# A hybrid decoder layer on one core: the recurrence's GELU, two weight sums, the turned rows and five joins in other places

## The chip, the cores and the metric

The kernel runs on one core of a Trainium2 chip. The metric is the device time of one execution in microseconds; where several runs of a kernel are given, their median stands. The engines are TensorE (PE, its weight loads PEld), VectorE (DVE), ScalarE (ACT), GpSimd (POOL), and SyncE (SP), which here issues most transfers.

## The reference

One layer of a decoder on 512 tokens of width 2048, in float32. Two mixers run side by side on the normalized input: a gated linear recurrence of 1024 channels behind a short convolution, and a head group of RWKV type (16 heads of 64). Then come a gated feed-forward net of width 6144 with a convolution over three tokens in its gate, a gated embedding, and a last norm:

```
xb = causal_dwconv(z[..., :D_LRU], conv_a_w, conv_a_b)
yb = gelu(z[..., D_LRU:2 * D_LRU])
out_a = rmsnorm(rg_lru(xb, ...) * yb, lru_norm)
...
h = h + concatenate([out_a, out_b], -1) @ w_o
u = rmsnorm(h, ln_ffn)
gate = causal_dwconv(u @ w_gate, conv_f_w, conv_f_b)
h = h + (gelu(gate) * (u @ w_up)) @ w_down
u = rmsnorm(h, ln_ple)
e = sigmoid(u @ w_ple_gate) * (p @ w_ple_proj)
h = h + rmsnorm(e, ln_ple_post)
return rmsnorm(h, ln_final)
```

## The kernel before

Every large product is made of three matmuls on two halves of the float32 operands: a weight tile `wraw` or `x` is split into `whi` (ScalarE, L138) and the rest `wlo` (VectorE, L139), and TensorE sums high times high, low times high and high times low. Where a weight is a sum of blocks (below), the sum comes first.

Phase 1 holds the mixers. It is written as generators whose pieces a scheduler orders by priority: `high_priority(offset=...)` moves an instruction up on the engines. For each of 4 head groups of the recurrence two blocks (i = 0, 1) of 128 channels pass through `lru_y` (L1013). Its dense product goes into a PSUM bank of two, named `mm`. VectorE empties the bank into `y` (L1021), ScalarE takes the GELU (L1022), and for i = 0 the gates' matmuls follow (L1031 to L1035), each emptied by ScalarE (L1038). Then come the exponential, tanh and square root of the recurrence (L1044 to L1046), POOL's product (L1050), VectorE's scan (L1051) and the product with `y` (L1052), which goes to `oa` in DRAM (L1053) and is read back later as `row` and `lx`. GELU, square root and exponential each need another table in ScalarE; a change shows as ACT_TABLE_LOAD. The head group's own chain (`Tm`, `MQ`, `NQ`, `Tt`) runs between these on all engines.

Phase 2 starts with the output projection, the hidden state `hT` and, in `forms`, the operands `s` of a fast product. The state goes to `hd` in DRAM (L1287). The gate loop makes 48 blocks n of 128 columns, gate (even n) and up (odd n), p = n // 2 being the pair. A block has seven units, named p1, p4, p2, q5, p7, p6 and p3, each one sub-product with a weight that is a block of `wgu` or a sum of some. `gate_order` (L1122) gives their order, `gate_unit` (L1132) their weights. Blocks are loaded into `x0` to `x7` by SP (L1139), sums are made by VectorE (`add`, L1143) or by a POOL transfer that accumulates into `g["s"]` (L1160). Between the units of the first blocks the token sums of `hT` squared are made (L1278, L1279, then a matmul L202, POOL's root L206, a broadcast L215).

A gate block is scaled (L1346) and convolved into the buffer x9 (ScalarE L1349, VectorE L1351, GELU L1352); the next up block is multiplied by it (L1433) and `spill` writes it out. The 16 rows of the hidden state are also turned here, for the later stages that want tokens on partitions: `row` is loaded from `hd` (L1414), transposed in place on 32 by 32 tiles (L1404) and written by four transfers to `hx` (L1407). One row is turned every 18 units from the 28th unit on.

After the down projection and the gated embedding the end handles four tiles tt of 128 tokens, in an order written by hand. The last gate product of each tile is on TensorE (L1590 to L1592); ScalarE and VectorE make its part of the embedding and its sums (L1699 to L1705), VectorE a mean (L1636), POOL a power (L1623). With the result r, `joined` (L1647) makes e r + h for four column blocks cb on VectorE (L1650), `rfin` (L1641 to L1644, again POOL's power) the last norm's factor, and `final` (L1652) scales each block, on ScalarE (L1655) or VectorE (L1657), and writes it out (L1658).

Of the kernel before, what the change touches and what calls it, by code (L numbers as in the profile page):

```python
# [7 lines left out]
ALU = mybir.AluOpType  # L8
# [82 lines left out]
class Builder:  # L91
# [921 lines left out]
    def lru_y(self, n, i):  # L1013
# [7 lines left out]
        V.tensor_tensor(y, ps, self.rs, ALU.mult)  # L1021
        SC.activation(y, y, AF.Gelu_apprx_tanh)  # L1022
# [17 lines left out]
        with self.tc.high_priority(offset=W['offl']):  # L1040
            tx, t1 = self.lgate[2 * i:2 * i + 2]

            rc = T("lrc")
            SC.activation(rc, t1, AF.Exp, scale=self.dv("m4sp", m), bias=self.dv("m4sp", m))  # L1044
            SC.activation(t1, t1, AF.Tanh, scale=self.dv("m2sp", m), bias=self.dv("m2sp", m))
            SC.activation(t1, t1, AF.Sqrt, scale=-0.25)  # L1046
            V.scalar_tensor_tensor(t1, rc, 1.0, t1, ALU.add, ALU.mult)
            G.memset(t1[:, 0:1], 0.5)
            V.scalar_tensor_tensor(tx, tx, 1.0, self.xc[i], ALU.add, ALU.mult)
            G.tensor_tensor(t1, t1, tx, ALU.mult)  # L1050
            V.tensor_tensor_scan(tx, rc, t1, 0.0, ALU.mult, ALU.add)  # L1051
            V.tensor_tensor(tx, tx, y, ALU.mult)  # L1052
            nc.sync.dma_start(self.oa[m], tx)  # L1053
            if m == 0:
                SC.activation(self.rsa, tx, AF.Square)
            else:
                SC.activation(rc, tx, AF.Square)
                V.tensor_tensor(self.rsa, self.rsa, rc, ALU.add)
# [72 lines left out]
    def gate_unit(self, n, u):  # L1131
# [22 lines left out]
        if u == "p7":  # L1154
            if n < 2:
                g[11] = load(2, 0, 0)
            return add(g[21], g[21], g[11])
        if u == "p6" and n in (0, NF - 1):
            return add(g["s"], g["s"], g[11])
        nc.gpsimd.dma_start(g["s"], src(0, 0 if u == "p6" else 1), accum_op=ALU.add)  # L1160
# [70 lines left out]
    def phase2(self):  # L1231
# [171 lines left out]
        def turn(m):  # L1403
            V.transpose(acc, acc)  # L1404
            for a in range(4):
                f = m % 4 * 128 + 32 * a
                nc.sync.dma_start(hx[m // 4][:, f:f + 32].rearrange("(b i) j -> i b j", i=32),  # L1407
                                  acc[32 * a:32 * a + 32].rearrange("i (b j) -> i b j", j=32))

        raw, c = [], None  # L1410
        for k, (n, u) in enumerate(self.gate_order()):
            m = k // 18 - 1
            if 0 <= m < KT and k % 18 == 6:
                nc.sync.dma_start(acc, hd[m // 2][:, m % 2])  # L1414
            if 0 <= m < KT and k % 18 == 10:
                turn(m)
# [3 lines left out]
            if n == 1 and u == "p6":  # L1420
                self.rstd_bcast(acc, D, RMS_EPS, k2, rs, rt)
                c = B(9)
                conv(0, o, c)
# [10 lines left out]
            raw.append(o)  # L1434
            if p % 2 == 1:
                spill(p // 2, raw)
                raw = []
# [213 lines left out]

        def final(tt, r, cb, act=True):  # L1652
            ix = tt * 4 + cb
            if act:
                SC.activation(e[ix], e[ix], AF.Copy, scale=r)  # L1655
            else:
                V.tensor_scalar(e[ix], e[ix], r, None, MU)  # L1657
# [30 lines left out]
        with self.tc.manual_schedule(engines={ET.PE, ET.DVE, ET.Activation, ET.Pool}):  # L1688
            for tt in range(4):
# [6 lines left out]

                sg, ee, x = T("e", 2, (128, 2, S))[:, 0], T("e", 2, (128, 2, S))[:, 0], e[tt * 4 + 3][:, last]
# [9 lines left out]
                if tt:  # L1707

                    joined(tt - 1, r, (3,))
                    for cb in range(4):  # L1710
                        final(tt - 1, rf, cb)
                r = rn
                joined(tt, r, (0,))
                rf = rfin(tt, r)
                joined(tt, r, (1, 2))
            joined(3, r, (3,))
            for cb in range(4):
                final(3, rf, cb, cb < 3)
# [67 lines left out]
```

## Time and profile before

| what | value |
|---|---|
| median of 3 runs | 2527.17 us (2523.64 to 2529.20) |
| the profiled execution's own time | 2528.72 us |
| its span (first to last instruction) | 2526.9 us |
| mean granted clock of TensorE | 0.992 |
| ScalarE's splits L138 of `x` | 332, mean 1061 ns |
| VectorE's splits L139 of `x` | 332, mean 1219 ns |
| accumulating transfers L1160 | 94 of 512 KB, median 5.7 us to land |

The profile is one execution. Each row of a timeline gives the start, the duration, the engine, the line, the operation, its output and inputs, and in brackets how long the engine had been idle and what ended that. A view of stretches gives the busy time of each engine in each, the clock that TensorE was granted (1.00 is full speed), and the share of its transfer engines that was busy. The rows on which the argument rests are in the prediction.

### The profile page before, as it was taken

What the parts mean: (1) busy time and instruction counts of PE and PEld (TensorE: products, weight loads), DVE (VectorE), ACT (ScalarE), POOL (GpSimd) and SP (SyncE); (2) the same over time, 40 slices, a digit from 0 to 9 for tenths busy, and PEclk for the clock granted to TensorE, in tenths of its full rate; (3) what the DMA queues carried; (4) which work ended last, traced back from release to release, by engine and by line L of the source; (5) the groups of instructions that cost most, each with busy time, mean ns of one, the idle gap of its engine ahead of it and who ended that gap; (6) DMA issues with size and microseconds to landing.
All of it is one profiled execution on the core that took longest, in us unless ns stands there. A gap on an engine that the chain in (4) does not pass through costs nothing.

```text
span 2526.9 us, 51719 instructions
## 1 busy us (share of the span) xinstructions
PE 2473.3 (98%) x21858; PEld 2182.3 (86%) x21858; DVE 1903.1 (75%) x2626; ACT 1250.0 (49%) x1735; POOL 220.3 (9%) x244
## 2 busy tenths in 40 slices
PE   9989999999999989999999999999999999999997
PEld 8867777777777889999999999999988888888887
DVE  5855775776585879878988888888877787896457
ACT  6563654556442545434444444444466454535345
POOL 0000100101031000000000000000000000000001
PEclk9999999999999999999999999999999999999998
DMA  7222222222342568888877777776788686853333
GB/s 260 89 78 63 88 77 65 88 81 68 102 131 93 161 198 218 203 212 221 211 196 176 204 194 193 203 196 176 213 250 234 172 264 188 254 130 117 100 92 109
DMA packets 168570, 402.17 MB, mean 159 GB/s; under 512 B 48529, under 2 KB 60817, under 8 KB 168337
## 3 DMA queue, kind: packets, MB, share of 16 engines
q1 hardware_dynamic: 133744, 307.62, 36.9%
q0 software_dynamic: 19872, 72.36, 17.3%
q10 hardware_dynamic: 14720, 18.88, 2.2%
q8 instruction: 171, 2.80, 0.5%
q14 instruction: 63, 0.51, 0.1%
HBM read 358.16 MB, written 40.63 MB: 158 GB/s over the span
## 4 chain that ended last, share of the span: by engine, by line
PE 60%; DVE 5%; DMA 3%; issue 2%; ACT 1%; POOL 0%; SPq 0%; POOLq 0%; ACTq 0%; DVEq 0%
PE mm L1304 7%; PE mm L1303 7%; PE mm L1302 7%; PE mm L1448 6%; PE mm L1447 6%; PE mm L1451 6%; PE wk L1302 3%; PE wk L1303 3%; PE wk L1304 3%; PE mm L1590 2%; PE mm L1591 2%; PE mm L1592 2%; PE mm L173 2%; PE mm L175 2%; PE mm L177 2%
## 5 line engine op out<-in xcount | busy, mean ns | idle before, releaser
L138 ACT ACTIVATE whi<-x 128x1024 fp32r<-128x1024 f32 x332 | 351.1, 1061 | 450.5 <-PE mm L1303 181.2
L139 DVE TENSOR_TENSOR wlo<-x,whi 128x1024 fp32r<-128x1024 f32 x332 | 404.7, 1219 | 120.4 <-ACT whi L138 116.5
L1302 PE MATMUL mm<-s,whi 128*128 128x256 f32 x1432 | 398.0, 278 | 4.5 <-ACT whi L138 3.6
L1304 PE MATMUL mm<-s,wlo 128*128 128x256 f32 x1432 | 398.3, 278 | 3.8 <-DVE wlo L139 3.7
L1303 PE MATMUL mm<-s,whi 128*128 128x256 f32 x1432 | 397.9, 278 | 0.0
L138 ACT ACTIVATE whi<-wraw 128x1024 fp32r<-128x1024 f32 (+1 forms) x223 | 227.0, 1018 | 341.7 <-PE mm L175 165.3
L139 DVE TENSOR_TENSOR wlo<-wraw,whi 128x1024 fp32r<-128x1024 f32 (+1 forms) x223 | 269.4, 1208 | 132.3 <-ACT whi L138 130.3
L173 PE MATMUL mm<-x,whi 128*128 128x512 f32 x832 | 332.5, 400 | 1.5 <-DVE hT L468 0.9
L177 PE MATMUL mm<-x,wlo 128*128 128x512 f32 x832 | 332.1, 399 | 0.0
L175 PE MATMUL mm<-x,whi 128*128 128x512 f32 x832 | 330.5, 397 | 0.0
L1302 PEld LDWEIGHTS mm<-s,whi 128*128 128x128 f32 x1432 | 270.6, 189 | 5.0 <-ACT whi L138 3.8
L1304 PEld LDWEIGHTS mm<-s,wlo 128*128 128x128 f32 x1432 | 270.0, 189 | 4.7 <-DVE wlo L139 4.7
L1303 PEld LDWEIGHTS mm<-s,whi 128*128 128x128 f32 x1432 | 270.1, 189 | 0.2
L1448 PE MATMUL mm<-whi,s 128*128 128x512 f32 x680 | 265.4, 390 | 0.9 <-DVE s L157 0.9
L1447 PE MATMUL mm<-whi,s 128*128 128x512 f32 x680 | 265.6, 391 | 0.0
L173 PEld LDWEIGHTS mm<-x,whi 128*128 128x128 f32 x832 | 157.1, 189 | 37.1 <-issue 2.7
L177 PEld LDWEIGHTS mm<-x,wlo 128*128 128x128 f32 x832 | 156.9, 189 | 34.0 <-issue 1.9
L175 PEld LDWEIGHTS mm<-x,whi 128*128 128x128 f32 x832 | 157.1, 189 | 33.7 <-issue 1.8
L1451 PE MATMUL mm<-wlo,s 128*128 128x512 f32 x680 | 181.3, 390 | 0.0
L1302 PE MATMUL wk<-s,whi 128*128 128x256 f32 x584 | 162.5, 278 | 2.0 <-ACT whi L138 2.0
L1304 PE MATMUL wk<-s,wlo 128*128 128x256 f32 x584 | 162.4, 278 | 0.4 <-DVE wlo L139 0.4
L1160 POOL DMA_DIRECT2D x<-wgu x94 | 82.7, 880 | 913.5 <-DVE wlo L139 663.9
(579 smaller groups left out, 5386.2 us busy)
## 6 DMA issues: line engine op xcount, KB each, us to landing
x<-wgu SPq DMA_DIRECT2D x144, 512.0 KB, 4.4
x<-wgu POOLq DMA_DIRECT2D x94, 512.0 KB, 5.7
wraw<-wz SPq DMA_DIRECT2D x80, 512.0 KB, 3.5
x<-wd SPq DMA_DIRECT2D x52, 512.0 KB, 6.0
wraw<-wgu SPq DMA_DIRECT2D x51, 512.0 KB, 4.6
x<-wd POOLq DMA_DIRECT2D x44, 512.0 KB, 6.0
wraw<-wpg SPq DMA_DIRECT2D x31, 512.0 KB, 3.5
rd<-x SPq DMA_DIRECT2D x24, 512.0 KB, 4.7
```

The source lines that it names most:

```text
L138: nc.scalar.activation(hi, raw, AF.Copy)
L139: nc.vector.tensor_tensor(lo, raw, hi.bitcast(F32), ALU.subtract)
L173: nc.tensor.matmul(ps, hi[:, k, :], xh, start=first and i == 0, stop=False)
L175: nc.tensor.matmul(ps, hi[:, k, :], xl, start=False, stop=False)
L177: nc.tensor.matmul(ps, lo[:, k, :], xh, start=False, stop=last and i == n - 1)
L1160: nc.gpsimd.dma_start(g["s"], src(0, 0 if u == "p6" else 1), accum_op=ALU.add)
L1302: TE.matmul(ps, wh[:, k, :], xh, start=k == 0, stop=False)
L1303: TE.matmul(ps, wh[:, k, :], xl, start=False, stop=False)
L1304: TE.matmul(ps, wl[:, k, :], xh, start=False, stop=k == 7)
L1447: TE.matmul(ps, x[0][:, k, ts_(tt)], w[0][:, k, :], start=first and k == 0, stop=False)
L1448: TE.matmul(ps, x[1][:, k, ts_(tt)], w[0][:, k, :], start=False, stop=False)
L1451: TE.matmul(ps, x[0][:, k, ts_(tt)], w[1][:, k, :], start=False, stop=last and k == 1)
```

## The change

It has four parts. In `lru_y` the evacuation L1021 gets the priority offset that the head group's evacuations have, and the GELU is written behind the recurrence's gates, ahead of the scan. In `gate_unit` the accumulating transfers of (0, p3) and (1, p6) become a plain load and a sum on VectorE; (1, p7) uses the block that (1, p6) has loaded. The turn of a row no longer works in place: it writes into the convolution's buffer x9 right after the multiply of each pair from p = 1 to 16, and the next row is loaded at once. At the end five joins (blocks 1 to 3 of tile 2, and 1 and 2 of tile 3) become ten float32 matmuls, of the identity with h and of a diagonal of r with e, into PSUM banks from which `final` reads.

```diff
 lru_y
-        V.tensor_tensor(y, ps, self.rs, ALU.mult)
-        SC.activation(y, y, AF.Gelu_apprx_tanh)
+        with self.tc.high_priority(offset=self.OFFS):
+            V.tensor_tensor(y, ps, self.rs, ALU.mult)
...
             G.tensor_tensor(t1, t1, tx, ALU.mult)
+            SC.activation(y, y, AF.Gelu_apprx_tanh)
             V.tensor_tensor_scan(tx, rc, t1, 0.0, ALU.mult, ALU.add)
 gate_unit
         if u == "p7":
-            if n < 2:
+            if n < 1:
                 g[11] = load(2, 0, 0)
             return add(g[21], g[21], g[11])
-        if u == "p6" and n in (0, NF - 1):
+        if u == "p6" and n in (0, 1, NF - 1):
+            if n == 1:
+                g[11] = load(2, 0, 0)
             return add(g["s"], g["s"], g[11])
+        if u == "p3" and n == 0:
+            return add(g["s"], g["s"], load(1, 0, 1))
 turned rows
         def turn(m):
-            V.transpose(acc, acc)
+            h = B(9)[:, 0]
+            V.transpose(h, acc)
+            if m + 1 < KT:
+                nc.sync.dma_start(acc, hd[(m + 1) // 2][:, (m + 1) % 2])
...
-            if 0 <= m < KT and k % 18 == 6:
-                nc.sync.dma_start(acc, hd[m // 2][:, m % 2])
-            if 0 <= m < KT and k % 18 == 10:
-                turn(m)
...
             raw.append(o)
+            if 0 < p <= KT:
+                turn(p - 1)
 the end
+        def onto(tt, cbs, stream):
+            for cb in cbs:
+                ix = tt * 4 + cb
+                if stream:
+                    sums[ix] = self.mm()
+                    TE.matmul(sums[ix], self.K("ident"), h3[ix], start=True, stop=False)
+                else:
+                    TE.matmul(sums[ix], diag[tt], e[ix], start=False, stop=True)
...
+                if tt == 3:
+                    onto(2, (1, 2, 3), True)
+                    onto(2, (1, 2, 3), False)
+                    onto(3, (1, 2), True)
...
-                    joined(tt - 1, r, (3,))
+                    if tt < 3:
+                        joined(tt - 1, r, (3,))
...
+                if tt >= 2:
+                    V.tensor_scalar(diag[tt], self.K("ident"), r, None, MU)
                 joined(tt, r, (0,))
                 rf = rfin(tt, r)
-                joined(tt, r, (1, 2))
+                if tt < 2:
+                    joined(tt, r, (1, 2))
             joined(3, r, (3,))
-            for cb in range(4):
-                final(3, rf, cb, cb < 3)
+            onto(3, (1, 2), False)
+            for cb in (0, 3, 1, 2):
+                final(3, rf, cb, cb < 2)
```

Three places show what the scheduler makes of it. The first is ScalarE in the last group of the recurrence, from the row L814 at 610.81 us of the profile on (`lxl` from `mm` is the row that empties the gates' bank). Before:

```order
L814 ACTIVATE ak_7911<-AR_7447 128x512
L138 ACTIVATE whi_7413<-wraw_7411 128x1024
L819 ACTIVATE ak_7911<-AR_7447 32x8x32 x4
L1038 ACTIVATE lt_1027_7435<-wk_7426,der 128x512
L944 ACTIVATE Sq_7444<-y_1029_7443 128x512
L1044 ACTIVATE lrc_7473<-lt_1027_7435,der 128x512
L672 ACTIVATE lhi_8362<-lraw_8357 128x384
L677 ACTIVATE lhi_8362<-lraw_8357 96x128
L1038 ACTIVATE lxl_1036_7462<-mm_7437,der 128x512
```

After the change:

```order
L814 ACTIVATE ak_7911<-AR_7446 128x512
L1051 ACT_TABLE_LOAD
L1051 ACTIVATE row_112<-row_112 128x512
L819 ACTIVATE ak_7911<-AR_7446 32x8x32 x4
L944 ACTIVATE Sq_7443<-y_1029_7442 128x512
L672 ACTIVATE lhi_8362<-lraw_8357 128x384
L677 ACTIVATE lhi_8362<-lraw_8357 96x128
L1038 ACTIVATE lxl_1036_7461<-mm_7436,der 128x512
L138 ACTIVATE whi_7412<-wraw_7410 128x1024
```

The table load and the GELU (L1022 before, L1051 now) stand ahead of the four `ak` rows, and the split of `whi`, the row `lt` from `wk` and the exponential `lrc` have moved behind the row that empties the bank.

The second is VectorE at the first gate units, from the row at 909.00 us on. Here x0 and x3 are the sums of units p7 and p6 of block 0, x4 and x7 those of block 1. Before:

```order
L1143 TENSOR_TENSOR x7_1584_10966<-x4_1582_10962,x5_1583_10964 128x1024
L160 SCALAR_TENSOR_TENSOR s27_1470_10139<-hT7_8340,par2_58,s27_1470_10139 128x256
L1143 TENSOR_TENSOR x4_1582_10962<-x4_1582_10962,x6_1599_11106 128x1024
L1279 TENSOR_TENSOR row_1442_10102<-row_1442_10102,rsa_86 128x512
L1143 TENSOR_TENSOR x0_1568_10855<-x0_1568_10855,x2_1574_10894 128x1024
L1279 TENSOR_TENSOR row_1442_10102<-row_1442_10102,rsa_86 128x512
L1143 TENSOR_TENSOR x3_1570_10859<-x3_1570_10859,x2_1574_10894 128x1024
L139 TENSOR_TENSOR wlo_1576_10898<-x0_1568_10855,whi_1575_10897 128x1024
L1279 TENSOR_TENSOR row_1442_10102<-row_1442_10102,rsa_86 128x512
L139 TENSOR_TENSOR x15_1566_10826<-wraw_1564_10823,x12_1565_10825 128x1024
L139 TENSOR_TENSOR wlo_1581_10934<-x3_1570_10859,whi_1580_10933 128x1024
```

After the change:

```order
L1144 TENSOR_TENSOR x7_1584_10966<-x4_1582_10962,x5_1583_10964 128x1024
L160 SCALAR_TENSOR_TENSOR s27_1470_10139<-hT7_8340,par2_58,s27_1470_10139 128x256
L1284 TENSOR_TENSOR row_1442_10102<-row_1442_10102,rsa_86 128x512
L1144 TENSOR_TENSOR x0_1568_10855<-x0_1568_10855,x2_1574_10894 128x1024
L1144 TENSOR_TENSOR x4_1582_10962<-x4_1582_10962,x6_1595_11070 128x1024
L1284 TENSOR_TENSOR row_1442_10102<-row_1442_10102,rsa_86 128x512
L139 TENSOR_TENSOR wlo_1576_10898<-x0_1568_10855,whi_1575_10897 128x1024
L1284 TENSOR_TENSOR row_1442_10102<-row_1442_10102,rsa_86 128x512
L139 TENSOR_TENSOR x15_1566_10826<-wraw_1564_10823,x12_1565_10825 128x1024
L1144 TENSOR_TENSOR x3_1570_10859<-x3_1570_10859,x2_1574_10894 128x1024
L1284 TENSOR_TENSOR row_1442_10102<-row_1442_10102,rsa_86 128x512
L139 TENSOR_TENSOR wlo_1581_10934<-x3_1570_10859,whi_1580_10933 128x1024
```

The sum of x4 has changed places with the sum of x0, so the latter is one sum nearer to the front; the second sum of x3 has gone behind the split of `wraw`, which stands at another place relative to the row sums L1279 (now L1284).

The third is VectorE at the end, from the last join of tile 1 (in both cases the first row) to the first row of tile 3's embedding (L1700). Before:

```order
L1650 SCALAR_TENSOR_TENSOR x_3611_25828<-x_3611_25828,row_25285,s_2884_22004 128x512
L1650 SCALAR_TENSOR_TENSOR s_3604_25821<-s_3604_25821,row_25285,x_2889_22009 128x512
L1641 SCALAR_TENSOR_TENSOR row_25285<-row_25285 128x1
L1642 SCALAR_TENSOR_TENSOR row_25285<-row_25285 128x1
L1643 SCALAR_TENSOR_TENSOR row_25285<-row_25285 128x1
L1644 TENSOR_SCALAR row_25285<-row_25285 128x1
L1650 SCALAR_TENSOR_TENSOR x_3605_25822<-x_3605_25822,row_25285,x_2890_22010 128x512
L1650 SCALAR_TENSOR_TENSOR s_3606_25823<-s_3606_25823,row_25285,x_2885_22005 128x512
L1700 SCALAR_TENSOR_TENSOR e_27376<-e_27375,x_3753_26783 128x256
```

After the change:

```order
L1656 SCALAR_TENSOR_TENSOR x_3628_25846<-x_3628_25846,row_25303,s_2901_22022 128x512
L1739 TENSOR_SCALAR row_25303<-con,row_25303 128x128
L1656 SCALAR_TENSOR_TENSOR s_3621_25839<-s_3621_25839,row_25303,x_2906_22027 128x512
L1647 SCALAR_TENSOR_TENSOR row_25303<-row_25303 128x1
L1648 SCALAR_TENSOR_TENSOR row_25303<-row_25303 128x1
L1649 SCALAR_TENSOR_TENSOR row_25303<-row_25303 128x1
L1650 TENSOR_SCALAR row_25303<-row_25303 128x1
L1724 SCALAR_TENSOR_TENSOR e_27406<-e_27405,x_3770_26801 128x256
```

Two joins between L1644 and L1700 are gone (L1650 and L1724 now), and the diagonal, L1739, stands ahead of the first join of tile 2.

More of the change, by code (lines that the diff above doesn't have):

```diff
@@ L1407, in turn @@
                 nc.sync.dma_start(hx[m // 4][:, f:f + 32].rearrange("(b i) j -> i b j", i=32),
-                                  acc[32 * a:32 * a + 32].rearrange("i (b j) -> i b j", j=32))
+                                  h[32 * a:32 * a + 32].rearrange("i (b j) -> i b j", j=32))
         raw, c = [], None
-        for k, (n, u) in enumerate(self.gate_order()):
-            m = k // 18 - 1
-            if 0 <= m < KT and k % 18 == 6:
-                nc.sync.dma_start(acc, hd[m // 2][:, m % 2])
-            if 0 <= m < KT and k % 18 == 10:
-                turn(m)
+        for n, u in self.gate_order():
             for m in late.get((n, u), ()):
@@ L1421, in phase2 @@
                 self.rstd_bcast(acc, D, RMS_EPS, k2, rs, rt)
+                nc.sync.dma_start(acc, hd[0][:, 0])
                 c = B(9)
@@ L1650, in joined @@
                 V.scalar_tensor_tensor(e[ix], e[ix], r, h3[ix], MU, AD)
+        sums = {}
+        diag = {tt: small(128) for tt in (2, 3)}
+        def onto(tt, cbs, stream):
[6 more added lines that the diff above has]
+                    TE.matmul(sums[ix], diag[tt], e[ix], start=False, stop=True)
         def final(tt, r, cb, act=True):
             ix = tt * 4 + cb
+            x = sums.get(ix, e[ix])
             if act:
-                SC.activation(e[ix], e[ix], AF.Copy, scale=r)
+                SC.activation(e[ix], x, AF.Copy, scale=r)
             else:
-                V.tensor_scalar(e[ix], e[ix], r, None, MU)
+                V.tensor_scalar(e[ix], x, r, None, MU)
             nc.sync.dma_start(A["out"][tt * 128:(tt + 1) * 128, cb * S:(cb + 1) * S], e[ix])
```

## The prediction

> **What bounds the kernel now.** The first view is the page: busy time by engine and the chain of work that ended last.
>
> ```profile
> PE 2473.3 (98%) x21858; PEld 2182.3 (86%) x21858; DVE 1903.1 (75%) x2626; ACT 1250.0 (49%) x1735; POOL 220.3 (9%) x244
> PE 60%; DVE 5%; DMA 3%; issue 2%; ACT 1%; POOL 0%; SPq 0%; POOLq 0%; ACTq 0%; DVEq 0%
> ```
>
> TensorE sets the end. The span of 2526.9 us holds 2473.3 us of it, so at most 53.6 us can come from filling its idle time, besides what a halved clock costs. A change to other engines counts only where TensorE stands still. The second view, busy time by stretches, shows where it does (columns: stretch, its length, busy us and instructions of PE, PEld, DVE, ACT, POOL, granted clock, DMA share, GB/s).
>
> ```profile
> 600.00:625.00 25.00, 22.45 (x196) 17.27 (x195) 15.85 (x29) 23.48 (x41) 4.07 (x6) 0.93 0.26 75
> 900.00:925.00 25.00, 22.07 (x167) 21.15 (x166) 20.80 (x28) 12.33 (x19) 1.08 (x1) 0.93 0.84 286
> 925.00:950.00 25.00, 20.58 (x157) 20.09 (x156) 16.46 (x22) 8.77 (x10) 4.69 (x4) 0.86 0.61 138
> 2500.00:2525.00 25.00, 10.33 (x90) 10.13 (x89) 19.26 (x51) 12.75 (x29) 7.30 (x8) 0.79 0.45 168
> ```
>
> These are the last recurrence blocks (600 to 650), the first gate units (900 to 950) and the end; a fourth place, the turned rows after 1083, is in part 3. Some stretches also ran at a lower clock. Cut finer:
>
> ```profile
> 643.80:647.21 3.41, 0.79 (x34) 0.44 (x36) 3.07 (x7) 0.67 (x2) 0.00 (x0) 1.00 0.12 25
> 647.21:650.62 3.41, 3.41 (x70) 2.79 (x58) 3.41 (x7) 1.64 (x2) 0.00 (x0) 0.50 0.86 269
> 913.46:916.87 3.41, 1.45 (x10) 1.05 (x9) 3.41 (x5) 3.13 (x4) 0.00 (x0) 1.00 0.94 298
> 916.87:920.28 3.41, 3.41 (x18) 3.41 (x17) 3.10 (x4) 0.98 (x2) 0.32 (x1) 0.50 0.90 290
> 1083.92:1087.33 3.41, 2.35 (x20) 2.35 (x21) 3.38 (x5) 0.99 (x2) 0.00 (x0) 1.00 0.61 102
> 1087.33:1090.74 3.41, 3.41 (x32) 3.41 (x32) 3.34 (x6) 1.06 (x1) 0.86 (x1) 1.00 1.00 384
> ```
>
> 3.41 us in which TensorE idled 2.62 us (3.41 less 0.79) or 1.96 us are followed by 3.41 us at clock 0.50; idle of 1.06 us is not. At half clock 3.41 us do 1.71 us of work, so one such stretch costs 1.7 us. I take the threshold between 1.06 and 1.96 us of idle per stretch. The Trainium skill, page "TensorE: Matmul & The Clock Gate", Part 1, has a free-running window of 3413 ns, and the stretches here agree in length. Its section "Why this matters for your kernels" asks only for no idle gaps above some 3 us; the drop after 1.96 us here speaks against that, and the measurement decides. By the page's rule the new gaps of the second part below could never halve the clock; by the rows one of them may, which is 1.7 us.
>
> **Part 1, the recurrence's GELU.**
>
> ```profile
> 611.54 0.50 PE L1031 MATMUL mm<-lxh,whi 128*128 128x512 f32 x1 [1.85 <-DVE row L1021]
> 616.56 0.67 ACT L1038 ACTIVATE lxl<-mm,der 128x512 f32<-128x512 f32 x1
> 617.28 0.50 PE L173 MATMUL mm<-x,whi 128*128 128x512 f32 x1 [0.19 <-ACT lxl L1038]
> 622.60 1.28 ACT L1022 ACT_TABLE_LOAD   x1
> 647.01 0.95 PE L843 MATMUL wk<-Tm,MQ 32*32 32x16 f32 x64 [2.62 <-DVE Tm L836]
> ```
>
> The evacuation L1021 moves up on VectorE, so the 1.85 us ahead of 611.54 go and the gates' matmuls end at about 613.4. But the next dense (L173, at 617.28) needs the bank that L1038 empties, and ScalarE runs without a pause here: a table load (1.28) and the GELU (0.63) now stand ahead of L1038, while a weight split (1.06 by its like in part 2) and two rows of the recurrence fall behind it. Added up row by row, L1038 ends at about 617.0. TensorE then idles 3.6 us and pays the half clock later: about 1.1 us behind at 620. Further on L836 no longer stands behind the scan; I get its end at 645.3, so that L843 starts 1.2 us sooner, and with TensorE late from 620 on the idle of 643.80 to 647.21 is gone, and the half clock behind it (1.7). After that VectorE waits for the rows that `oa` brings back, landing as before, and most is given back by 665. Bounds: -2.9 when nothing is given back, +1.1 when only the loss stays. I take **-0.5**, near the middle since the loads are the nearest wait. For the six earlier blocks the rows move nothing on TensorE's path: 0.
>
> **Part 2, the first gate units.**
>
> ```profile
> 907.45 0.51 PE L1302 MATMUL mm<-s,whi 128*128 128x256 f32 x2 [0.97 <-ACT s L156]
> 914.69 0.39 PE L1302 MATMUL wk<-s,whi 128*128 128x256 f32 x1 [0.72 <-ACT whi L138]
> 916.43 0.38 PE L1302 MATMUL wk<-s,whi 128*128 128x256 f32 x1 [1.24 <-ACT whi L138]
> 937.77 0.58 PE L1302 MATMUL mm<-s,whi 128*128 128x256 f32 x1 [3.58 <-ACT whi L138]
> 939.40 0.58 PE L1304 MATMUL mm<-s,wlo 128*128 128x256 f32 x1 [0.84 <-DVE wlo L139]
> 919.96 1.08 POOL L1160 DMA_DIRECT2D x<-wgu  x1 [93.57 <-DVE wlo L139]
> 945.51 2.03 POOL L206 TENSOR_TENSOR rsr<-rsm,mhalf 128x4 f32<-128x4 f32 x1 [0.77 <-DMA wraw<-wgu]
> 929.01 1.06 ACT L138 ACTIVATE whi<-x 128x1024 fp32r<-128x1024 f32 x1 [4.60 <-DMA x<-wgu]
> 934.76 1.06 ACT L138 ACTIVATE whi<-x 128x1024 fp32r<-128x1024 f32 x1 [4.18 <-DMA x<-wgu]
> 910.53 1.22 DVE L1143 TENSOR_TENSOR x<-x,x 128x1024 f32<-128x1024 f32 x1
> DMA to landing us min/median/max: 3.5/5.8/9.4
> ```
>
> TensorE idles 7.35 us here (the five brackets). The clocks of 0.93 and 0.86 from 900 to 950 lose 25 x 0.07 + 25 x 0.14 = 5.2 us, or three half stretches at 1.7, 5.1: 12.45 in all. ScalarE's splits stand in line behind two accumulating transfers; the first is issued at 919.96 and used at 929.01, the second used at 934.76. Both are replaced by a plain load and an add of 1.22 us on VectorE; the loads stand with the first ones of SP, which land by 911.
>
> By the new order, with the durations of these rows: the operand of (0,p7) is ready 1.2 us earlier, since the add of x6 (1.22) now stands behind it, so 914.69 and 916.43 become one gap of 1.05. Then TensorE runs to the token sums (0.45 behind VectorE's row sum) and to (0,p3), whose add stands behind that: 1.27 for ScalarE's split, 0.95 for the next split and the 2.03 us POOL row of the root. Last, (1,p2) to q5(2) wait for VectorE, which waits for x1: SP issues it only after that add, at 929.6, and with the median of 5.8 us to land (last row) TensorE idles 1.85. The 0.97 before 907.45 stays. The sum is 0.97 + 1.05 + 0.45 + 2.2 + 1.85 = 6.5 of idle (the 2.2 is what the three waits at (0,p3) leave open, since they run side by side). The 2.2 fall into two stretches; the 1.85 stand below the 1.96 that halved the clock. 12.45 less 6.5 is **-5.9**. The adds' 2.4 us hide in VectorE's idle (8.5 of 25 us in 925 to 950). Bounds: -9.5 when the three waits behind the sums are hidden too; -1 when x1 takes the 9.4 us of the slowest load, which adds 3.6 of idle and a half stretch.
>
> **Part 3, the turned rows.**
>
> ```profile
> 1083.11 0.71 DVE L1404 STREAM_TRANSPOSE row<-row 128x512 f32<-128x512 f32 x1 [5.18 <-DMA row<-hd]
> 1084.98 0.38 PE L1304 MATMUL mm<-s,wlo 128*128 128x256 f32 x1 [1.80 <-DVE wlo L139]
> 1165.88 0.39 PE L1304 MATMUL mm<-s,wlo 128*128 128x256 f32 x1 [1.05 <-DVE wlo L139]
> 1093.60 0.49 SPq L1407 DMA_DIRECT2D hx<-row  x1
> DMA to landing us min/median/max: 1.9/4.5/9.7
> 1349.11 1.22 DVE L1433 TENSOR_TENSOR x<-x,x 128x1024 f32<-128x1024 f32 x1
> 1369.41 1.52 ACT L1349 ACTIVATE x<-x,par 128x512 f32<-128x512 f32 x2 [1.04 <-DVE x L1346]
> ```
>
> VectorE stood 5.18 us before a transpose, with a split of weights behind it that TensorE needed. The row is now fetched right behind the transpose before, some 38 us ahead, so the wait goes; 16 transposes of 0.71 stay. **-2.85** (1.80 and 1.05). The bounds are 0, where some other row is late next, and -3.2. The new place costs nothing as long as the four hx writes have read the buffer of the convolution before it is written again.
>
> **Part 4, the end.**
>
> ```profile
> 2514.34 0.74 DVE L1650 SCALAR_TENSOR_TENSOR s<-s,row,x 128x512 f32<-128x512 f32 x1
> 2515.00 0.42 DVE L1700 SCALAR_TENSOR_TENSOR e<-e,x 128x256 f32<-128x256 f32 x1
> 2518.03 0.75 DVE L1650 SCALAR_TENSOR_TENSOR s<-s,row,x 128x512 f32<-128x512 f32 x1 [0.43 <-POOL row L1623]
> L741 DVE TENSOR_SCALAR bdr<-con,par x8: 246/286/287, 25.2 to 661.5; 128x128 f32<-128x128 f32 x8
> L273 PE MATMUL wk<-y x4: 1061/1061/1220, 1.5 to 4.2; 128*128 128x512 f32 x4
> ```
>
> The last matmul ends at 2510.33 (the 10.33 us that TensorE has in the stretch from 2500); then VectorE is the chain. Two joins (0.66 apart) leave it ahead of L1700; a diagonal comes in (0.29 by L741, 0.2 net of overlap): -1.1. The third join lay under POOL's power and frees nothing, the second diagonal adds 0.2. The finals are split two and two, so the last output is issued about 0.45 sooner. Sum **-1.35**. The ten matmuls of TensorE start 0.85 apart by the L273 rows (four starts in 1.5 to 4.2): 8.5 us from 2510.33 to about 2518.9, ahead of the last power's end. Bounds: 0 and -1.9; were all ten at half clock they would end at 2527, and the time rises by some 5.
>
> **Sum.** -0.5 - 5.9 - 2.85 - 1.35 = -10.6. The profiled run took 2528.72 (its span and 1.8 around it), so it would take 2518.1. That run lies 1.55 above the median of three, 2527.17, which makes **2516.6**.
>
> **Rivals.** *Only the old waits change their names*: part 2's gain is taken by x1's late landing and part 1's by the loads. Against it: the accumulations were in series, which no new load is. It leaves parts 3 and 4 and 1 us, -5.2: 2522. Chance 0.15. *Everything behind the sums is hidden as well*, and part 1 gives nothing back: -2.9 - 9.5 - 3.2 - 1.9 = -17.5, or 2510. Chance 0.15. *Slower: the convolution's buffer.* ScalarE's first row of each convolution now waits for the hx writes issued after the transpose. It stands in ScalarE's line ahead of the splits. From the transpose, behind the multiply of 1349.11 and one split, to that row at 1369.41 lie about 17 us. From the transpose of 1083.11 to the landing of its last write (issued at 1093.60, 4.5 to land) the trace needed 14, with SP held by other transfers. Beyond 17 us each microsecond is paid at 16 convolutions: 2 us more make +32 against -7.75 from parts 1, 2 and 4, or 2551. For it: the 14. Against it: the writes now stand ahead of the dd writes on SP. Chance 0.05. *The change does not act*, since the order hardly differs where TensorE waits: 2527. The rows of the order show that it does differ; 0.05. My own case has the remaining 0.6.
>
> **Range and chances.** A measurement of this kernel tells about 0.2%, 5 us, from no change. The range takes in the second and third cases and most of the bounds: 2508 to 2525. Faster by over 5 us (below 2522) takes 0.56 of my case's 0.6, the good one's 0.15 and half of the first rival: 0.78. Within 0.2% are the rest of these and the case without effect: 0.04 + 0.08 + 0.04 = 0.16; slower: 0.06.
>
> **What would show it.** Part 1: no gap at 609.7, a gap of over 3 us near 613.4 with half clock after it, none at 645. Part 2: no split of ScalarE waiting over 4 us for a transfer near 929, and 925 to 950 above 22 us busy. Part 3: no idle of TensorE in 1083 to 1166, and no wait of the convolution's first row for a transfer. Part 4: the last join's place taken by the diagonal, and TensorE done by 2519 at full clock. Wrong would be a half clock near 930, or a gap after x1.

## The result, and the profile after

| kernel | median us | runs | ratio to before (95% interval) |
|---|---|---|---|
| before | 2529.20 (2523.64 to 2530.92) | 5 | 1 |
| changed | 2512.12 (2508.65 to 2516.77) | 5 | 0.9939 [0.9922, 0.9956] |

The change makes the kernel faster by 15.4 us (2529.2 less 0.9939 times it), with an interval from 11 to 20. The forecast was 10.6 us less. In the two profiled executions, 2528.72 and 2511.03 us, the spans are 2526.9 and 2509.3, 17.6 apart. The first view of after is the page again: its busy times and the chain that ended last.

```profile
PE 2473.0 (99%) x21878; PEld 2178.1 (87%) x21878; DVE 1906.5 (76%) x2626; ACT 1253.8 (50%) x1735; POOL 218.7 (9%) x242
PE 66%; DVE 3%; ACT 1%; issue 1%; DMA 1%; POOL 0%; POOLq 0%; ACTq 0%; DVEq 0%
```

TensorE's busy time is as before, though the span is shorter by 17.6 us, and that equality misleads. The changed kernel holds the ten added matmuls, 8.6 us of busy time behind the last gate product (2493.51 to 2502.10). Everywhere else its busy time fell by about 9 us, because matmuls that start far apart, or run at half clock, count as busy all the while. So the gain lies partly in idle time and partly in busy time. VectorE's and the transfers' shares of the chain fell (5% to 3%, 3% to 1%). The second view is that of stretches, at the places of part 1 and part 2.

```profile
600.00:625.00 25.00, 20.90 (x190) 16.26 (x189) 15.37 (x28) 21.87 (x38) 3.10 (x4) 0.93 0.23 74
614.27:617.68 3.41, 0.00 (x0) 0.00 (x0) 1.46 (x4) 3.35 (x9) 0.00 (x0) 1.00 0.00 0
618.83:622.24 3.41, 3.41 (x12) 2.75 (x10) 2.28 (x3) 3.18 (x6) 0.00 (x0) 0.50 0.56 126
649.55:652.96 3.41, 1.76 (x76) 1.37 (x76) 2.74 (x6) 1.85 (x3) 0.00 (x0) 1.00 0.62 164
652.96:656.37 3.41, 3.41 (x10) 2.64 (x9) 2.70 (x6) 0.00 (x0) 0.00 (x0) 0.50 0.61 190
900.00:925.00 25.00, 23.20 (x184) 22.32 (x183) 23.40 (x34) 13.44 (x22) 0.00 (x0) 1.00 0.77 279
925.00:950.00 25.00, 23.96 (x200) 23.35 (x199) 20.28 (x26) 10.95 (x14) 2.98 (x3) 1.00 0.59 149
```

At 614 the loss that the prediction named is there, with its half clock. A second half clock stands at 652.96 (before, at 647.21). From 900 to 950 TensorE works 47.16 of 50 us, not 42.65, and no half clock is left.

The lag of after behind before, taken at the same matmul of both, says where the 17.6 us lie. It is +1.3 us at 508 us (a half clock near 189 that lasted two stretches instead of one, where the two kernels still do the same), +1.6 at 682, +1.7 at 901, -6.3 at 973, the same at 1031, then -15.8 at 1269 and -16.8 when the last gate product ends. So the largest piece, 9.5 us, fell between 1031 and 1269: the turned rows, where 2.85 were forecast. The third view is the list of what VectorE waited for between 940 and 1280 us: line, releaser, us in all, times, longest. Before:

```profile
DVE row L1404 <- DMA row<-hd: 16.9, 8, 5.2
DVE wlo L139 <- ACT whi L138: 13.1, 12, 2.0
DVE row L1404 <- issue: 9.1, 3, 4.3
DVE row L1404 <- DMA x<-wgu: 4.5, 1, 4.5
```

After:

```profile
DVE wlo L139 <- ACT whi L138: 24.8, 19, 3.6
DVE x L1340 <- PE mm L1309: 8.3, 16, 0.6
```

No transpose waits any more; 30.5 us of VectorE's standing ahead of transposes are gone. The transposes of the two kernels, from the view of one line (count, shortest, median and longest ns, first and last start), show why there were so many. Before:

```profile
L1404 DVE STREAM_TRANSPOSE row<-row x16: 702/711/715, 960.2 to 1200.1; 128x512 f32<-128x512 f32 x16
```

After:

```profile
L1410 DVE STREAM_TRANSPOSE x<-row x16: 705/706/708, 992.5 to 1564.3; 128x512 f32<-128x512 f32 x16
```

Before, the scheduler had drawn the sixteen turns together, 16.0 us apart ((1200.1 - 960.2) / 15), however the program spreads them. Load, transpose and writes all used one buffer, so they had to follow each other, and it seems to be this chain that sets the pace (argued, not tested). After the change they stand 38.1 us apart.

TensorE's visible waits between 1031 and 1269 were 3.2 us before (1.80, 0.35, 1.05) and none after. That is a third of the 9.5. The rest is in the spacing of the matmuls, which busy time doesn't show. Stretches of 25 us before:

```profile
1050.00:1075.00 25.00, 25.00 (x223) 25.00 (x223) 19.97 (x25) 12.01 (x14) 2.01 (x3) 1.00 0.82 195
1185.00:1210.00 25.00, 25.00 (x214) 25.00 (x214) 20.99 (x26) 11.49 (x12) 2.63 (x3) 1.00 0.92 225
1210.00:1235.00 25.00, 25.00 (x214) 25.00 (x213) 22.47 (x26) 11.96 (x13) 2.46 (x3) 1.00 0.74 182
```

One of them after:

```profile
1185.00:1210.00 25.00, 25.00 (x223) 25.00 (x222) 21.10 (x25) 12.45 (x14) 2.65 (x3) 1.00 0.81 213
```

All are busy 25.00 of 25.00 at clock 1.00, but 214 matmuls fit in where 223 could: one starts every 0.1178 us (called wide from here on) instead of every 0.1133 (narrow). Each count takes in two or three matmuls that overlap the edges, and the overlapping records make both stretches look full. A wide stretch costs about 1 us in 25 (9 x 0.1133). Before, three such stretches stand between 1093 and 1242. Each began at a late weight load; the first two ended at the next wait, the third without any delay. This is one such start, TensorE's timeline with its weight loads (PEld):

```profile
1093.15 0.28 PE L1303 MATMUL mm<-s,whi 128*128 128x256 f32 x1
1093.27 0.35 PE L1304 MATMUL mm<-s,wlo 128*128 128x256 f32 x1
1093.45 0.28 PE L1302 MATMUL mm<-s,whi 128*128 128x256 f32 x1
1093.57 0.28 PE L1303 MATMUL mm<-s,whi 128*128 128x256 f32 x1
1093.69 0.28 PE L1304 MATMUL mm<-s,wlo 128*128 128x256 f32 x1
1093.81 0.28 PE L1302 MATMUL mm<-s,whi 128*128 128x256 f32 x1
```

```profile
1092.93 0.19 PEld L1302 LDWEIGHTS mm<-s,whi 128*128 128x128 f32 x1
1093.05 0.19 PEld L1303 LDWEIGHTS mm<-s,whi 128*128 128x128 f32 x1
1093.23 0.19 PEld L1304 LDWEIGHTS mm<-s,wlo 128*128 128x128 f32 x1
1093.34 0.19 PEld L1302 LDWEIGHTS mm<-s,whi 128*128 128x128 f32 x1
```

The load for L1304 starts 0.18 behind the one ahead of it, not 0.11 or 0.12; its matmul takes 0.35, and from then on the starts stand 0.12 apart. Of the 2014 intervals between 1031 and 1269, 1046 are 0.116 to 0.14 long before and 48 after. Summed over what they exceed 0.1133 by, the wide ones cost 4.7 us before and 0.2 after, those over 0.3 us long 4.0 and 0, and those between these lengths 1.1 and 0: 9.7 us in all, against 0.2. (In every kernel a third spacing, 0.1167, stands for some 8 us near 987, 1226 and 1531, with no late load; it is the 0.2, and the third wide stretch of before ran into it.)

How the loss divides changes from one execution to the next. The kernel with the joins alone (below) gives each engine the same instructions in the same order as before until 2512 us. It lost 9.1 us over the same matmuls, but with only 1.3 us of wide spacing, and with a half clock at 1092 that before doesn't have.

### The profile page after: what moved, and what is told of

Read it like the earlier page. It is cut to its first block, busy times and chain, and to the rows that moved or that the text cites. A ratio compares the mean times of both kernels' runs of the same rounds, so it can differ in the third digit from the quotient of the medians.

```text
span 2509.3 us, 51757 instructions
## 1 busy us (share of the span) xinstructions
PE 2473.0 (99%) x21878; PEld 2178.1 (87%) x21878; DVE 1906.5 (76%) x2626; ACT 1253.8 (50%) x1735; POOL 218.7 (9%) x242
## 4 chain that ended last, share of the span: by engine, by line
PE 66%; DVE 3%; ACT 1%; issue 1%; DMA 1%; POOL 0%; POOLq 0%; ACTq 0%; DVEq 0%
PE mm L1307 8%; PE mm L1309 8%; PE mm L1308 8%; PE mm L1453 6%; PE mm L1454 6%; PE mm L1457 6%; PE wk L1307 3%; PE wk L1309 3%; PE wk L1308 3%; PE mm L1596 2%; PE mm L1598 2%; PE mm L1597 2%; PE mm L173 2%; PE mm L177 2%; PE mm L175 2%
## 5 line engine op out<-in xcount | busy, mean ns | idle before, releaser
L1307 PE MATMUL wk<-s,whi 128*128 128x256 f32 x584 | 161.5, 277 | 0.4 <-ACT whi L138 0.4
L1308 PE MATMUL wk<-s,whi 128*128 128x256 f32 x584 | 161.3, 276 | 0.0
```

The lines of the kernel that those rows point to most:

```text
L1307: TE.matmul(ps, wh[:, k, :], xh, start=k == 0, stop=False)
L1308: TE.matmul(ps, wh[:, k, :], xl, start=False, stop=False)
```

## The experiments

My theory after this reading was this: part 3 is worth about 9.5 us by itself, since late weight loads cost TensorE twice, as waits and as the wide spacing behind them; part 2 is worth some 8 us, but only if the turned rows don't take it back. Each kernel of the first four is the kernel before with one part of the change.

**The turned rows alone.**

```diff
-            V.transpose(acc, acc)
+            h = B(9)[:, 0]
+            V.transpose(h, acc)
+            if m + 1 < KT:
+                nc.sync.dma_start(acc, hd[(m + 1) // 2][:, (m + 1) % 2])
...
+            if 0 < p <= KT:
+                turn(p - 1)
```

> The kernel before with the turned rows alone moved. Theory pace: the late row did more than the 3.2 us of visible gaps; behind each late weight split TensorE goes on with matmuls 0.1178 us apart instead of 0.1133 for tens of us (before: most of 1093 to 1247), so this part alone is worth 9.5 us (ratio 0.9963) and the blocks of 256 columns stand 19.04 us apart from 1030 on. Rival gaps only: 3.2 us (0.9987), and the wide spacing stays in 1093 to 1247. In the profile the lag against before should go from about 0 at 950 to -9.5 at 1270 by the first, to -3.2 by the second.

Measured: 2521.10 us against 2530.57, ratio 0.9963 [0.9950, 0.9976], -9.4 us. The lag behind before goes from +2.1 at 1031 to -7.4 at 1269, the same 9.5 us as in the whole change. The rival's 3.2 us would be 0.9987, outside the interval. From 973 to 1269 this kernel, the changed one, the two parts together, the one with three times the writes and the last version (all below) take the same time to within 0.1 us. The part changes the buffer, the place of the turn and the load at once, and no run separates these. The stretch from 1185 to 1210 of this kernel is at the narrow spacing:

```profile
1185.00:1210.00 25.00, 25.00 (x223) 25.00 (x222) 19.54 (x22) 10.35 (x11) 2.63 (x3) 1.00 0.79 213
```

**The two sums alone.**

```diff
-            if n < 2:
+            if n < 1:
                 g[11] = load(2, 0, 0)
...
-        if u == "p6" and n in (0, NF - 1):
+        if u == "p6" and n in (0, 1, NF - 1):
+            if n == 1:
+                g[11] = load(2, 0, 0)
...
+        if u == "p3" and n == 0:
+            return add(g["s"], g["s"], load(1, 0, 1))
```

> The kernel before with the two sums alone (load and add in place of the accumulating transfers). Theory: 5.9 us by the prediction's sum of idle and half clock, up to 8 with what the trace of the changed kernel shows between 908 and 973 (ratio 0.9968 to 0.9977); the 3.58 us gap at 934 and the 6.83 us at half clock go. Rival: the gain needs the turned rows gone from SP's line too, then under 3 us. The wide spacing behind 1093 must stay.

Measured: 2526.61 us, ratio 0.9984 [0.9972, 0.9996], which is 4 us less (1 to 7). That is below the 5.9 to 8 of the theory and above the rival's 3. In the profiled execution, which at 2530.84 is slower than the median, the lag falls from +0.4 at 901 to -6.9 at 973, and stands at +1.8 at 1269: there, all of it is given back. Over the runs it can't be all, since the median does gain. In the timeline of this kernel TensorE and VectorE still wait at the old turned rows:

```profile
1043.68 0.39 PE L1308 MATMUL mm<-s,x 128*128 128x256 f32 x1 [1.61 <-DVE x L139]
1124.75 0.71 DVE L1408 STREAM_TRANSPOSE row<-row 128x512 f32<-128x512 f32 x1 [4.90 <-DMA row<-hd]
```

Its stretches have the wide spacing, 215 matmuls in 25 us:

```profile
1185.00:1210.00 25.00, 25.00 (x215) 25.00 (x214) 19.85 (x25) 10.74 (x12) 2.66 (x3) 1.00 0.84 213
```

So part 2's gain was no sure sum: what TensorE gains there, it can spend waiting for the next late row. In the kernels with the old rows the same matmuls from 973 to 1269 took longer than in the changed kernel by 9.5 us (before), 9.1 (joins alone), 14.8 (GELU alone) and 18.2 (sums alone), one execution of each.

**The GELU alone.**

```diff
-        V.tensor_tensor(y, ps, self.rs, ALU.mult)
-        SC.activation(y, y, AF.Gelu_apprx_tanh)
+        with self.tc.high_priority(offset=self.OFFS):
+            V.tensor_tensor(y, ps, self.rs, ALU.mult)
...
+            SC.activation(y, y, AF.Gelu_apprx_tanh)
             V.tensor_tensor_scan(tx, rc, t1, 0.0, ALU.mult, ALU.add)
```

> The kernel before with the GELU and its evacuation alone moved. Theory: the 1.85 us gap at 609.7 turns into a gap of 3.6 us before the next dense product behind L1038, with the half clock moved behind it; 0 to +1.0 us in all (ratio 1.0000 to 1.0004). Rival: worth 0.5 to 2.9 us as the better Tm chain suggests (0.9989 to 0.9998). The stretch from 500 to 540 gains 0.6 us in both.

Measured: 2530.86 us, ratio 1.0005 [0.9992, 1.0018]; the lag is -2.0 at 508, -2.8 at 541 and -1.8 at 682. So an earlier group gains 0.8 and the last one loses 1.0. The time can't tell this from the rival's gain: its interval reaches 2 us down. The wait moved as forecast:

```profile
614.27 0.50 PE L173 MATMUL mm<-x,whi 128*128 128x512 f32 x1 [3.56 <-ACT lxl L1038]
```

**The joins alone.** The edit is the change's last part, `onto`, `diag` and the order of the last `final`s.

> The kernel before with the five joins alone moved to TensorE. Theory: 0.8 to 1.4 us (ratio 0.9995): 1.1 us at the last L1700, then part is lost since the last output of tile 2 is issued late. Rival: nothing, since the float32 matmuls end after the last power. From the end of the last gate matmul to the end of the span there should be 15.2 to 15.8 us instead of 16.6.

Measured: 2532.23 us, ratio 1.0000 [0.9984, 1.0015]. The profiled run takes 15.75 us from the end of the gate products to the end of the span, where before took 16.62: it gains 0.9 us there. The time can't tell that from nothing.

**Sums and rows together**, without GELU and joins (the two edits shown above).

> The kernel before with parts 2 and 3 alone (the two weight sums and the turned rows; GELU and joins stand as before). My theory: with the turned rows in the new place the sums' gain is kept behind 1031 us, and the two parts make the result nearly alone: -8 us between 900 and 975 us of the profile, -9 us between 1031 and 1270, and -1.5 to -2.5 at 1840 to 1870, so 2512.5 to 2515 us against 2530, ratio 0.9930 to 0.9945. Rival (each part is worth what it gives alone, and the rest of the change carries the difference): the two single ratios 0.9984 and 0.9963 multiply to 0.9947, with -2 for the sums behind 1031, some 2517 us.

Measured: 2513.74 us against 2529.66, ratio 0.9937 [0.9925, 0.9949]. The span is 2510.7 (before 2526.9, so -16.2); the whole change, at 2509.3, is 1.4 shorter, and that is all that is left to the other two parts and to chance. The rival's 0.9947 lies inside the interval too, so the time alone doesn't decide. In the profiled execution the lag is -6.3 at 974 us and -15.8 at 1326, with nothing given back; that speaks for the theory.

The next question was what makes the wide spacing. Its rivals were the rows' transfers and a late weight load.

**Three times the rows' writes**, in the changed kernel.

```diff
-            for a in range(4):
+            for a in range(4 * (3 if m < 8 else 1)):
+                a %= 4
```

> The changed kernel with the four writes of each of the rows 0 to 7 issued three times (same data, same place), so eight more transfers per row between 992 and 1262 us. Rival (the rows' transfers, by the memory port or by traffic, widen TensorE's spacing): 0.1178 us and 42 to 43 matmuls in 5 us in these blocks, some 0.7 us more for each 19 us block. Theory (only a late weight load does it): 0.1133 and 44 as in the changed kernel, wherever no weight split came late; the total within 0.1% of the changed kernel.

Measured: 2512.04 us, ratio 0.9933 [0.9913, 0.9952]. The spacing stays narrow, with the transfer engines as busy as in the wide stretches before:

```profile
1185.00:1210.00 25.00, 25.00 (x223) 25.00 (x222) 19.24 (x22) 10.02 (x11) 2.65 (x3) 1.00 0.95 237
```

So the number of these writes is not the cause (two runs, with one profile).

**Long reductions on VectorE**, in the changed kernel.

```diff
             V.transpose(h, acc)
+            if 5 < m < 13:
+                with self.tc.high_priority(offset=2 * W['offw']):
+                    w = 2 * m - 10
+                    V.tensor_reduce(acc[:, 0:w].unsqueeze(2), h.unsqueeze(1).broadcast_to([128, w, S]),
+                                    mybir.AxisListType.X, ALU.add)
```

> The changed kernel with one long VectorE reduction (2, 4, ... 14 times 512 elements, estimated 1.1 to 7.5 us by 1.22 us for 1024 elements) behind the transposes of rows 6 to 12, some 1221 to 1450 us; its result is overwritten by the next row, so nothing is left out. VectorE's splits stand behind it, as they stood behind the waiting transpose before; there 5.2 us of wait made a stall of 1.8, so the longer four should stall TensorE by 0.9, 2, 3 and 4 us. Theory (a late weight load leaves TensorE at the wide spacing): behind several of these stalls the matmuls start 0.1178 us apart, 42 to 43 in 5 us at granted clock 1.00, for 10 us or more, where the changed kernel has 0.1133 and 44. Rival (the wide spacing comes of the turned rows' transfers or the place of their loads): 0.1133 and 44 directly behind every stall and its half clock; the loss is the stalls and half clocks alone.

Measured: 2520.36 us, ratio 0.9965 [0.9948, 0.9982]. Only the last two reductions stalled TensorE, and behind both the spacing was narrow; behind the half clock that followed the first it was wide for 4 intervals. The first stall in TensorE's timeline:

```profile
1418.91 0.38 PE L1309 MATMUL mm<-s,x 128*128 128x256 f32 x1 [3.08 <-DVE x L139]
```

The stretch of 25 us behind it has 223 matmuls again:

```profile
1425.00:1450.00 25.00, 25.00 (x223) 25.00 (x222) 22.58 (x28) 11.97 (x13) 2.68 (x3) 1.00 0.65 174
```

This miss took the theory's first form away: not every late load leaves the wide spacing.

**Reductions tuned to be just late**, in two sizes.

```diff
+            if 3 < m < 14:
...
+                    w = (21 if m % 2 == 0 else 17) + (m - 4) // 2
+                    V.tensor_reduce(acc[:, 0:w].unsqueeze(2), h[:, 0:256].unsqueeze(1).broadcast_to([128, w, 256]),
+                                    mybir.AxisListType.X, ALU.add)
```

> The changed kernel with a VectorE reduction behind the transposes of rows 4 to 13 (1145 to 1490 us), as in the run with the long reductions, but tuned to make the next weight split late by little: 17 to 21 times 256 elements behind odd rows, 21 to 25 behind even ones, estimated 4.6 to 6.7 us by the reductions of that run (1.209 us for 1024 elements, 7.611 for 7168); its result is overwritten by the next row. There 6.4 us behind an odd row made a stall of 3.08, 7.5 behind an even row 1.84, and neither left a wide spacing behind it. Theory, narrowed (the spacing can change at a small disturbance of TensorE's weight loads, of 0.05 to 0.4 us, and then stays until the next one): behind one or more of these ten the matmuls start 0.1178 us apart for over 10 us at granted clock 1.00, more than 8.3 us longer than the stretches of that length that every kernel has near 1226 and 1531. Rival (it needs something that the old place of the rows has, which is neither transfers nor late splits): at no place a wide stretch of over 8.3 us, only the stalls.

> The same with two more times 256 elements behind every row (19 to 23 odd, 23 to 27 even, estimated 5.1 to 7.2 us), so that the stalls are longer by about 0.5 us and other rows come just late. Theory, narrowed: again at least one wide stretch of over 10 us, at other rows; rival: none.

Measured: 2534.06 us, ratio 1.0006 [0.9989, 1.0023], and with the longer ones 2543.67, 1.0045 [1.0026, 1.0063]. Two late splits in TensorE's timeline of the first:

```profile
1268.82 0.39 PE L1309 MATMUL mm<-s,x 128*128 128x256 f32 x1 [0.83 <-DVE x L139]
1350.45 0.39 PE L1309 MATMUL mm<-s,x 128*128 128x256 f32 x1 [1.89 <-DVE x L139]
```

The stretches ahead of, between and behind them:

```profile
1240.00:1265.00 25.00, 25.00 (x223) 25.00 (x222) 24.90 (x30) 12.43 (x15) 2.66 (x3) 1.00 0.75 191
1275.00:1300.00 25.00, 25.00 (x214) 25.00 (x214) 22.77 (x27) 12.09 (x14) 2.67 (x3) 1.00 0.70 180
1355.00:1380.00 25.00, 25.00 (x223) 25.00 (x222) 22.26 (x28) 11.87 (x13) 2.26 (x3) 1.00 0.66 172
```

Behind the stall of 0.83 the spacing is wide for 82 us, until the next stall of 1.89; a second stretch begins at a stall of 0.90 at 1473 and runs, through one more stall, to 1551. There it meets the spacing of 0.1167 that every kernel has, and behind that, from 1558, it is narrow without any stall. In the other kernel two stand at 1234 to 1276 and 1320 to 1359, each begun behind a late split or its half clock and ended by the next late one. So a late weight load can put TensorE into the wide spacing, and another can end it: shown. It takes neither the rows' old place nor their old buffer. It can also end without one: the stretch to 1551 does, as does the last one of before. Of the 19 stalls of 0.25 us or more in these three runs (2, 7 and 10, those within 2 us counted as one) four left a stretch of over 10 us. Which stall does is open.

**A version with the losses of parts 1 and 4 taken out.**

```diff
 lru_y
+        if n == 3:
+            SC.activation(y, y, AF.Gelu_apprx_tanh)
...
-            SC.activation(y, y, AF.Gelu_apprx_tanh)
+            if n < 3:
+                SC.activation(y, y, AF.Gelu_apprx_tanh)
 final
-            nc.sync.dma_start(A["out"][tt * 128:(tt + 1) * 128, cb * S:(cb + 1) * S], e[ix])
+            q = nc.scalar if ix == 11 else nc.sync
+            q.dma_start(A["out"][tt * 128:(tt + 1) * 128, cb * S:(cb + 1) * S], e[ix])
```

The evacuation's higher priority, too, is left to the first three groups.

> The change with two edits: in the last recurrence group the GELU stands where it stood before, and the output block (tile 2, block 3) is issued by ScalarE behind the activation that makes it, not by SP behind a block that is ready 2.3 us later. By part 1's sum in the profile (+0.9 at the last group, -0.66 in the earlier ones) the first gives -0.9 or, where the clock's window falls otherwise, nothing; the second takes one issue of 0.4 to 0.5 us out of the five at the end. So 0 to -1.4 us against the changed kernel: ratio to the kernel before 0.9933 to 0.9939, below what the measurement can tell from the change. Rival (the late issue costs nothing, as the landing of the last block ends the run): last landing at the same distance from the last scaling as in the changed kernel, 4.3 us from the start of the last VectorE scaling to the last landing's end.

Measured: 2508.85 us, ratio 0.9919 [0.9907, 0.9932], span 2507.4. It is the fastest of all, clearly faster than before; its lead over the changed kernel (0.9939) is inside the intervals. In the profile both edits do their part: between 541 and 684 us it gains 1.1 us on the changed kernel, since neither half clock of part 1 is left, and the last block is issued 1.5 us behind the start of the last scaling on VectorE (2502.22 and 2503.73), not 2.0. From that start to the last landing it takes 4.2 us, and 4.9 in the changed kernel, so the rival of an equal distance falls; its 4.3 is not what the changed kernel has.

## Why the prediction was right, and where its terms were off

The forecast was 2516.6, the median 2512.12: faster, as the likeliest case said, and inside the range. That the range of 17 us took it in was partly luck, since the largest gain lay far outside its own bounds. The second rival's 2510 is nearer than the forecast, but not by its terms: part 1 gave no 2.9 us, and part 3 gave 9.5, not 3.2. The terms, against the lags of the profiled runs:

| term | forecast | measured |
|---|---|---|
| part 1, GELU | -0.5 | +0.3 (-0.6 from 508 to 541, +0.9 behind) |
| part 2, sums | -5.9 | -8.0 |
| part 3, turned rows | -2.85 | -9.5 |
| part 4, joins | -1.35 | -0.9 |
| not forecast: before 508 us | 0 | +1.3 |
| not forecast: 1841 to 1870 us | 0 | -1.5 |

**Part 3 was mis-sized**, "-2.85 (1.80 and 1.05)". The mechanism was right: VectorE stood before a transpose with a split behind it. But the sum took the two largest visible waits for the whole. The same queue cost 3.2 in visible waits, and about 6 more in short delays and in the wide spacing, which no row of idle time shows. The prediction's first premise, that a change to other engines "counts only where TensorE stands still", is what failed here: TensorE was busy for those 6 us. Its bound, -3.2, was too narrow for the same reason. The signs that were forecast held: TensorE is never idle between 1083 and 1166, and the convolution's rows on ScalarE (48, by the view of their line) wait for VectorE alone, 24 times, never visibly for the writes out of x9. The slower rival did not come.

**Part 2** came out 2.1 us better. The idle left at the first gate units, TensorE's waits after:

```profile
908.73 0.50 PE L1307 MATMUL mm<-s,whi 128*128 128x256 f32 x2 [0.58 <-ACT s L156]
916.54 0.38 PE L1309 MATMUL wk<-s,wlo 128*128 128x256 f32 x1 [1.22 <-DVE wlo L139]
```

with two more, 0.59 and 0.44, at 932. So 0.97 became 0.58, 1.05 became 1.22, the three waits at (0,p3) left 1.03 and not 2.2, and two terms never showed: the token sums' 0.45, and the 1.85 behind x1. SP did issue x1 when forecast (929.90 against 929.6), but TensorE had work in hand until it was used. That is 2.83 us of idle instead of 6.5, 3.7 less. Not all of it arrived: the half clocks before had cost 3.9 there (39 matmuls 0.213 apart instead of 0.1133), not the 5.1 that I took, and the short delays grew by 0.4 us between 901 and 973. That makes 3.7 less 1.2 less 0.4. As the prediction asked, 925 to 950 is above 22 us busy, and no half clock stands near 930.

**Part 1** was right at 614: a gap of 3.58 (forecast 3.6), with its half clock, and no gap at 609.7. It was wrong at 645: L843 no longer waits 2.62, but the stretch before 652.96 holds two later waits, 0.47 and 1.18, and the half clock that should have been saved comes there. It also put the earlier blocks at nothing, while in the changed kernel TensorE gains 0.6 us between 508 and 541, and 0.8 with the GELU alone.

**Part 4.** The joins take 0.86 us each on TensorE (three in 2493.35 to 2495.93; forecast 0.85), done by 2502.10 at full clock, ahead of the end of the last power at 2502.47, and the diagonal stands where a join stood. TensorE's rows at the end (each added matmul is recorded as two; those that join `mm<-s` lie between these rows):

```profile
2493.35 2.74 PE L1666 MATMUL mm<-x,con 128*128 128x512 f32 x6
2495.93 1.02 PE L1668 MATMUL mm<-x,row 128*128 128x512 f32 x2
2498.50 1.88 PE L1666 MATMUL mm<-x,con 128*128 128x512 f32 x4
2501.08 1.02 PE L1668 MATMUL mm<-x,row 128*128 128x512 f32 x2
```

That the price came out is luck. Line 273, from which it was read, issues two matmuls at the start of the kernel, recorded as four rows whose last three starts are 0.85 apart, so one took 1.7 us there, twice what it takes at the end. At that pace the ten would have taken 17 us, which is the case that the prediction feared. Why the first ones were slow isn't shown: the record of the granted clock begins behind them, at 5.51 us.

The size was off by SP, which the sum had not looked at. Its issues after:

```profile
2500.21 0.41 SPq L1677 DMA_DIRECT2D out<-s  x1
2503.03 0.33 SPq L1677 DMA_DIRECT2D out<-x  x1
2503.45 1.37 SPq L1677 DMA_DIRECT2D out<-s  x3
2504.91 0.51 SPq L1677 DMA_DIRECT2D out<-x  x1
```

The block `out<-x` of tile 3, ready at 2503.0, stands ahead of the last block of tile 2, ready at 2500.75; so five issues, not four, are left for the end, and one costs 0.4 to 0.5.

**Not forecast.** At 1866 us TensorE waited 0.73 for a split of the hidden state (L157) before and not after; with smaller ones that makes 1.5. This wait comes and goes among the kernels (0.56 and 0.85 with the rows alone, one of 0.17 with sums and rows), and what decides it is open. The 1.3 us before 508 are a half clock of two stretches instead of one. No edit acts before 509, yet the lags of the kernels at 508 range from -2.9 to +3.1, so this is a difference of executions, not of the change.

## What to carry to other kernels

Where one engine splits or loads for another, a wait on it should be priced by all the small lateness that it spreads, not only by the gaps that it leaves. Compare the number of matmuls in equal stretches, at busy 100% and full clock, with the best stretch of the same product. Look up where the scheduler really put a repeated step before pricing its waits; here the program spread sixteen turns over the loop, and the scheduler had packed them. A gain ahead of a chain of transfers is kept only if that chain isn't the next thing waited for, so two parts may be worth more together than apart; the profiled executions show it here, the times alone do not.

## What the runs showed of the hardware that was not expected

- TensorE has two lasting spacings for the 128x256 matmuls at granted clock 1.00: 0.1133 us (223 in 25 us) and 0.1178 (214). A late weight load can start the wide one, and it then held for up to 82 us. What holds it is not shown. In four kernels it ran into the third spacing, 0.1167, without another late load (before at 1242, the sums alone at 1244, the GELU alone at 1246, the shorter of the tuned reductions at 1551), and each time the narrow one stood behind it. The Trainium skill, page "TensorE: Matmul & The Clock Gate", says in Part 2, section "Back-to-back issue gap", that in a stream of weight loads and matmuls the spacing is set by both; that agrees with a spacing which changes where a weight load is late, but the page has no second steady value.
- Idle time in a stretch of 3.41 us is not by itself what halves the clock. In the changed kernel 1.65 us of idle (3.41 less 1.76, the rest mostly 32x16 matmuls) halved the next stretch. In the last version 1.75 us of idle (3.42 less 1.67) with 128x512 matmuls left it whole. In the profile before, the first two rows here, 0.45 us of idle (3.41 less 2.96) was enough, with products of 128x2, 64x64 and 32x32 from 333.92 on:

```profile
333.19:336.60 3.41, 2.96 (x56) 2.42 (x55) 0.96 (x3) 3.33 (x6) 1.45 (x1) 1.00 0.44 153
336.60:340.01 3.41, 3.15 (x63) 2.84 (x64) 2.21 (x5) 3.36 (x7) 0.18 (x1) 0.50 0.02 6
615.03:618.45 3.42, 1.67 (x8) 1.05 (x7) 2.68 (x5) 3.39 (x8) 0.00 (x0) 1.00 0.05 10
618.45:621.86 3.41, 3.41 (x20) 2.97 (x21) 2.12 (x4) 3.38 (x5) 0.00 (x0) 1.00 0.61 223
```

So the prediction's threshold, between 1.06 and 1.96 us of idle, is no rule for every stretch; it was contradicted by the profile before. For stretches with matmuls of 256 columns and more alone it holds, and the runs narrow it: 1.75 us left the clock whole (last version, and 615.71 to 619.12 with sums and rows), 1.79 halved it (917.57 to 920.98 with the joins alone). Small products seem to count for less than their busy time; the size of the product is the difference that these stretches show, and no run varied it alone.
